# Where an expert's third block does its activation, and three small branches in place of one in the first three experts

## The chip, the cores and the metric

The kernel runs on one core of one Trainium2 chip. The metric is device time in microseconds (us), from three runs; the profile shows one further execution. Line numbers (L1286) are those of the kernel before.

## The reference, cut to what matters

Two blocks of a transformer run one after the other on 256 tokens of width 1024. The first block ends in a mixture of 32 experts: a router picks four experts for each token, and each expert computes, for its tokens only,

```python
hdn = xb @ w_gate_up[e] + b_gate_up[e]          # 1024 -> 2048
x_glu = jnp.minimum(hdn[..., :1024], 7.0)
x_lin = jnp.clip(hdn[..., 1024:], -7.0, 7.0)
a = x_glu * sigmoid(1.702 * x_glu) * (x_lin + 1)
y = a @ w_down[e] + b_down[e]                    # 1024 -> 1024
out[token] += y * gate
```

All weights are float32, 12 MiB for an expert. The second block (two feed-forward layers and a mixer) follows and is not touched by the change.

## The kernel before

The experts run in a loop that is unrolled over e = 0 to 31. An expert's weights come in six chunks of 2 MiB: gate-up chunks ("gu", e, 0 to 3), each 256 input rows, and down chunks ("dn", e, 0 and 1), each 512 rows. The chunks go through a ring of nine slots, eight from the second expert's down chunks on. SyncE (SP) issues their loads in a fixed order. `release(key)` tells the ring, at that place of the program, that a chunk has been read; `fill()` then writes the load that takes over the slot into SP's queue, and on the chip that load waits until TensorE (PE) has passed the last instruction that reads the old chunk. A load thus starts only after the chunk eight places ahead of it has been read for the last time in the program's order, whichever branch was taken.

How many tokens an expert has is known only on the chip. PE, ScalarE (ACT) and VectorE (DVE) each read the count v and branch:

- v at most 32: the small way (`many.Else()`), here called few: 32 rows, four column groups of PE at a time (`gate_up_q`, `act_q`, `down_s`).
- v over 32: the main way, here called many: 64 rows, two column groups (`gate_up`, `act`, `actT`, `down`).
- v over 64 (`SL`): many, and in an inner branch a third block for tokens 65 to 96 (`gather_q`, `gate_up_q`, `act_q`, `down_q`, `combine`). (Experts with over 96 tokens have a loop of their own, `rounds`, which this input does not enter.)

In the profiled execution experts 9, 13 and 20 have a third block; 0, 3, 4, 6, 11, 12, 14, 19 and 23 are many without one; the other twenty are few.

An expert has two branches. The first holds gate-up chunks 0 to 2 (for e = 0 to 2 it is three branches, one for each chunk). Between the branches the next expert's rows are gathered (L1114). The second holds gate-up chunk 3, the activation, `between()` (the next expert's transposes and the sums of a finished pair of experts), and both down chunks; in an expert with over 64 tokens the third block's remainder comes behind the main down product: gate-up rows 6 and 7 of the eight (L1259), its activation, its one-hot rows (`slots_q`, DVE) and their transposes (`sgT`), a down product of 32 instructions 512 columns wide in the one shared PSUM buffer "rot" (L1315), a copy, and eight products into the sums (L1221). Only behind the whole second branch stand `release` for gate-up chunk 3 and both down chunks:

```python
        release(("gu", e, 3))
        for j in range(2):
            release(("dn", e, j))
```

An inner branch that is not taken is stepped over; PE then counts its semaphores as though the branch had run.

Of the kernel before, what the change touches and what calls it, by code (L numbers as in the profile page):

```python
# [95 lines left out]
def build(tc, A, out, dbg=None):  # L96
# [115 lines left out]
    def chunk(key):  # L212
        return tiles[index[key]]
# [910 lines left out]
    def sgT(Sg, r=0, pool=None):  # L1124
# [3 lines left out]
        s = (pool or pe).tile([128, T], F32, name="SgT" + ("z" if r else ""), bufs=1)  # L1128
# [57 lines left out]
    def down(e, py, at, r=0):  # L1186
        for c in range(2):
# [10 lines left out]
        if r:  # L1198
            y = pe.tile([128, 512], F32, name="yz", bufs=1)
            nc.scalar.activation(y, py, AF.Copy)  # L1200
            return y

# [33 lines left out]
    def gather_q(e, xe, p):  # L1236
# [5 lines left out]
        x = pe.tile([128, T], F32, name="SgTz", bufs=1)  # L1242
# [28 lines left out]
    def down_s(e, at, py):  # L1271

        lse = sel[0:96, e:e + 1].to_broadcast([96, 32])
        for g in range(4):
            nc.tensor.matmul(py[32 * g:32 * g + 32, 0:T], lhsT=lse, rhs=bg[0:96, 2048 + T * g:2048 + T * g + T],
                             start=True, stop=False, skip_group_check=True)
        l = yield
# [4 lines left out]
        for c in range(2):  # L1282
            w = chunk(("dn", e, c)).rearrange("p (k f) -> p k f", k=4)
            for j in range(4):
                for g in range(4):
                    nc.tensor.matmul(py[32 * g:32 * g + 32, 0:T], lhsT=at[:, j, 32 * c:32 * c + 32],  # L1286
                                     rhs=w[:, j, T * g:T * g + T], start=False, stop=(c == 1 and j == 3),
                                     skip_group_check=True)
        o = 64 * (e % 2)
        for g in range(4):  # L1290
            d, q = pair["y"][o:o + 32, T * g:T * g + T], py[32 * g:32 * g + 32, 0:T]
# [4 lines left out]
        yield  # L1296

    def down_q(e, l):
        p = ps.tile([128, 4, 64], F32, name="rot", bufs=1)
        for j in range(4):  # L1300
            nc.tensor.transpose(p[:, j], l[:, 128 * j:128 * j + 128], ident[0:64, 0:64])
        at = pe.tile([128, 4, 64], F32, name="aTq")
        nc.scalar.activation(at, p, AF.Copy)
        st = sgT(slots_q(e, 4, [128, 2, 128], "Sgz", 1), 1)
        p = ps.tile([128, 512], F32, name="rot", bufs=1)
        lse = sel[0:96, e:e + 1].to_broadcast([96, 32])
        for o in range(2):
            nc.tensor.matmul(p[64 * o:64 * o + 32], lhsT=lse, rhs=bg[0:96, 2048 + 512 * o:2560 + 512 * o], start=True,
                             stop=False, skip_group_check=True)
        for j in range(4):  # L1310
            for o in range(2):
# [742 lines left out]
```

## Time and profile before

| what | value |
|---|---|
| time, median of 3 runs | 1770.94 us (1769.97 to 1772.21) |
| the profiled execution, its own time | 1769.94 us |
| its span, first to last instruction | 1768.1 us |
[...]
| PE, DVE, ACT busy | 85%, 44%, 30% |
| HBM read | 545.25 MB, 309 GB/s over the span |

PE's share is an average over stages with different limits. The stage of the experts runs from about 213 to 1196 us, the second block from there to the end. The row of GB/s in 40 slices (44.2 us each) shows in which of them the loads set the pace. A wait "<-issue" is time in which the engine waited for nothing that the profile shows. [...]

### The profile page before, as it was taken

The page shows a single profiled execution, that of the slowest core. Times are in us where ns is not written, and L with a number is a line of the kernel's source. Part 1 is how long each engine was busy: PE and PEld are TensorE (multiplying, and loading weights), DVE is VectorE, ACT ScalarE, POOL GpSimd, SP SyncE. Part 2 cuts the span into 40 slices and gives each one's busy share as a digit, 9 for nine tenths or more (in the row PEclk, how much of TensorE's full clock was granted, in tenths as well). Part 3 has the DMA queues.
Part 4 walks back from the last instruction along what each step waited for, and adds up shares of the span by engine and source line. Part 5 has one row for each costly group of instructions (what it writes and reads, how often), then busy time and mean ns, then how long its engine had stood idle before and what let it go on. Part 6 is the DMA issues. An engine that isn't in the chain of part 4 may idle for free. (4 is left out here: it accounts for less than half of the span.)

```text
span 1768.1 us, 26974 instructions
## 1 busy us (share of the span) xinstructions
PE 1501.6 (85%) x10842; PEld 984.5 (56%) x10842; DVE 779.3 (44%) x1605; ACT 522.3 (30%) x1114; POOL 106.5 (6%) x114
## 2 busy tenths in 40 slices
PE   6999978967779888778868776668999999999998
PEld 5787623323233332332323222227999989999997
DVE  5776613233332432433211111115766767676665
ACT  4544311101011010110101101005544556565444
POOL 3501100000000000000000000002000100310000
PEclk8999999998999999999979888889999999999999
DMA  9878779999999979999999999995554553344630
GB/s 353 323 229 340 277 271 414 417 415 416 416 401 412 413 290 366 415 415 417 406 383 402 409 416 416 416 414 218 191 205 159 193 201 144 143 165 170 221 137 25
DMA packets 89049, 549.49 MB, mean 311 GB/s; under 512 B 5064, under 2 KB 7912, under 8 KB 49448
## 3 DMA queue, kind: packets, MB, share of 16 engines
q1 hardware_dynamic: 88424, 544.55, 77.9%
q8 instruction: 154, 2.52, 0.6%
q0 software_dynamic: 272, 0.92, 0.2%
q10 hardware_dynamic: 144, 1.05, 0.2%
q14 instruction: 55, 0.45, 0.1%
HBM read 545.25 MB, written 1.25 MB: 309 GB/s over the span
## 5 line engine op out<-in xcount | busy, mean ns | idle before, releaser
L251 DVE TENSOR_TENSOR wl<-ring,wh 128x512 fp32r<-128x512 f32 x421 | 284.9, 710 | 114.8 <-ACT wh L250 108.1
L250 ACT ACTIVATE wh<-ring 128x512 fp32r<-128x512 f32 x424 | 248.7, 622 | 106.5 <-PE gu L281 86.1
L1259 PE MATMUL h<-ring,xe 128*32 128x512 f32 x1280 | 194.5, 733 | 56.4 <-DMA ring<-in_w_gate_up 32.4
L280 PE MATMUL gu<-ring,wh 128*128 128x256 f32 x704 | 201.2, 286 | 2.9 <-ACT ring L1586 2.9
L281 PE MATMUL gu<-ring,wh 128*128 128x256 f32 x704 | 200.4, 285 | 1.9 <-DVE ring L1590 1.9
L282 PE MATMUL gu<-ring,wl 128*128 128x256 f32 x704 | 200.4, 285 | 0.0
L1155 PE MATMUL h<-ring,xe 128*64 128x512 f32 x768 | 173.6, 594 | 11.4 <-DMA ring<-in_w_gate_up 9.8
L1259 PEld LDWEIGHTS h<-ring,xe 128*32 128x32 f32 x1280 | 50.4, 127 | 181.5 <-issue 145.8
L1264 DVE TENSOR_SCALAR glu<-h 64x512 f32<-64x512 f32 x23 | 15.7, 683 | 287.5 <-PE h L1259 287.5
L280 PEld LDWEIGHTS gu<-ring,wh 128*128 128x128 f32 x704 | 135.9, 193 | 3.5 <-ACT ring L1586 3.3
L281 PEld LDWEIGHTS gu<-ring,wh 128*128 128x128 f32 x704 | 135.9, 193 | 2.2 <-DVE ring L1590 2.1
L282 PEld LDWEIGHTS gu<-ring,wl 128*128 128x128 f32 x704 | 135.9, 193 | 0.0
L1117 ACT ACTIVATE xg<-rot 128x512 f32<-128x512 f32 x28 | 16.7, 597 | 381.4 <-PE rot L1114 381.4
L1155 PEld LDWEIGHTS h<-ring,xe 128*64 128x64 f32 x768 | 56.6, 137 | 113.1 <-issue 96.5
L280 PE MATMUL pd<-acth,wh 128*128 128x256 f32 x352 | 98.8, 281 | 0.1
L281 PE MATMUL pd<-actl,wh 128*128 128x256 f32 x352 | 98.3, 279 | 0.1
L282 PE MATMUL pd<-acth,wl 128*128 128x256 f32 x352 | 98.2, 279 | 0.0
L1286 PE MATMUL h<-ring,aT 128*32 128x256 f32 x1280 | 78.2, 394 | 21.2 <-ACT aT L1281 10.7
L1195 PE MATMUL h<-ring,aT 128*64 128x512 f32 x384 | 86.7, 605 | 6.4 <-ACT aT L1175 6.4
L1372 DVE COPY_PREDICATED bias<-bm,vecs 128x512 f32<-128x512 uint8 x124 | 80.0, 726 | 1.1
L1160 DVE TENSOR_SCALAR glu<-h 128x512 f32<-128x512 f32 x12 | 8.3, 692 | 160.6 <-PE h L1155 160.6
L280 PE MATMUL gu<-big_h,wh 128*128 128x256 f32 x256 | 74.6, 291 | 0.0
(446 smaller groups left out, 2450.2 us busy)
## 6 DMA issues: line engine op xcount, KB each, us to landing
ring<-in_w_gate_up SPq DMA_DIRECT2D x127, 2048.0 KB, 23.2
ring<-in_w_down SPq DMA_DIRECT2D x62, 2048.0 KB, 24.6
ring<-in_ffn_gu SPq DMA_DIRECT2D x22, 2048.0 KB, 8.0
ring<-in_win SPq DMA_DIRECT2D x12, 2048.0 KB, 8.2
ring<-in_ffn_wd SPq DMA_DIRECT2D x10, 2048.0 KB, 9.5
ring<-in_ada SPq DMA_DIRECT2D x8, 2048.0 KB, 11.5
ring<-in_wout SPq DMA_DIRECT2D x4, 2048.0 KB, 7.8
ring<-in_ada SPq DMA_DIRECT2D x4, 1024.0 KB, 12.4
```

The source lines that it names most:

```text
L250: nc.scalar.activation(dh, src, AF.Copy)
L251: (eng or nc.vector).tensor_tensor(dl, src, dh.bitcast(F32), op=OP.subtract)
L280: nc.tensor.matmul(o, lhsT=wh, rhs=mh, start=start, stop=False, skip_group_check=True)
L281: nc.tensor.matmul(o, lhsT=wh, rhs=ml, start=False, stop=False, skip_group_check=True)
L282: nc.tensor.matmul(o, lhsT=wl, rhs=mh, start=False, stop=stop, skip_group_check=True)
L1117: nc.scalar.activation(x, p, AF.Copy)
L1155: nc.tensor.matmul(p[64 * hf:64 * hf + 64], lhsT=x, rhs=wk[:, 512 * hf:512 * hf + 512], start=False, stop=(k == KD - 1), skip_group_check= ...
L1195: nc.tensor.matmul(py[64 * oh_:64 * oh_ + 64], lhsT=at[:, j, 64 * c:64 * c + 64], rhs=wk[:, 512 * oh_:512 * oh_ + 512], start=False, stop= ...
L1259: nc.tensor.matmul(p[32 * g:32 * g + 32], lhsT=x(k), rhs=w[:, k % 2, c], start=False, stop=(k == KD - 1), skip_group_check=True)
L1264: nc.vector.tensor_scalar(g, p[0:64], 7.0, None, op0=OP.min)
L1286: nc.tensor.matmul(py[32 * g:32 * g + 32, 0:T], lhsT=at[:, j, 32 * c:32 * c + 32], rhs=w[:, j, T * g:T * g + T], start=False, stop=(c == 1 ...
L1372: nc.vector.copy_predicated(bias2[:, h], m, val[:, :, None].to_broadcast([128, 2, T]))
```

## The change

For every expert: the third block's gate-up rows 6 and 7 and its activation move from behind the main down product to just behind the main activation; its one-hot rows with their transposes move into the first branch, behind gate-up rows 0 to 5; its down product is made by the few way's routine, in quarters: 64 instructions of 256 columns in four column groups, written into the third block's own PSUM buffer `pq` instead of "rot"; chunk dn 0 is read wholly before dn 1; its copy and its sums work on 256 columns and 32 rows.

For e = 0 to 2 alone: the second branch becomes three, one up to the activation's transposes, and one for each down chunk, with a `release` behind each. For e above 2 there is one second branch as before, with two inner branches in it instead of one.

```diff
-    def sgT(Sg, r=0, pool=None):
+    def sgT(Sg, r=0, pool=None, s=None):
...
-        s = (pool or pe).tile([128, T], F32, name="SgT" + ("z" if r else ""), bufs=1)
+        if s is None:
+            s = (pool or pe).tile([128, T], F32, name="SgT" + ("z" if r else ""), bufs=1)
...
-        x = pe.tile([128, T], F32, name="SgTz", bufs=1)
+        x = pe.tile([128, 512], F32, name="yz", bufs=1)[:, 0:T]
...
+    def down_q(e, at, p, cs):
+
+        for c in cs:
             w = chunk(("dn", e, c)).rearrange("p (k f) -> p k f", k=4)
             for j in range(4):
                 for g in range(4):
-                    nc.tensor.matmul(py[32 * g:32 * g + 32, 0:T], lhsT=at[:, j, 32 * c:32 * c + 32],
+                    nc.tensor.matmul(p[32 * g:32 * g + 32, 0:T], lhsT=at[:, j, 32 * c:32 * c + 32],
                                      rhs=w[:, j, T * g:T * g + T], start=False, stop=(c == 1 and j == 3),
                                      skip_group_check=True)
...
-        st = sgT(slots_q(e, 4, [128, 2, 128], "Sgz", 1), 1)
-        p = ps.tile([128, 512], F32, name="rot", bufs=1)
...
-        for j in range(4):
-            for o in range(2):
-                for c in range(2):
-                    w = chunk(("dn", e, c)).rearrange("p (k f) -> p k f", k=4)
-                    g = 64 * o + 32 * c
-                    nc.tensor.matmul(p[g:g + 32], lhsT=at[:, j, 32 * c:32 * c + 32],
-                                     rhs=w[:, j, 512 * o:512 * o + 512], start=(c == 1 and j == 0), stop=(j == 3),
-                                     skip_group_check=True)
+    def combine_q(p, s):
         y = pe.tile([128, 512], F32, name="yz", bufs=1)
-        nc.scalar.activation(y, p, AF.Copy)
-        return y, st
+        nc.scalar.activation(y[:, 0:T], p[:, 0:T], AF.Copy)
+        for k in range(KD):
+            g, i = k // 2, k % 2
+            nc.tensor.matmul(acc[k], lhsT=y[32 * g:32 * g + 32, 128 * i:128 * i + 128], rhs=s[32 * g:32 * g + 32, :],
+                             start=False, stop=False, skip_group_check=True)
...
                     gate_up_q(e, further, pq, ks)
+                    if js[-1] == 2:
+                        sgT(slots_q(e, 4, [128, 2, 128], "Sgz", 1), 1, None, sz)
...
-        with tc.If(v > 32) as many:
+        def many_a():
             gate_up(e, xe, pg, pl_, (3,))
             a = act(pg, pl_)
+            with tc.If(v > SL):
+                gate_up_q(e, further, pq, range(6, 8))
+                act_q(pq, lq)
             between()
             down_bias(e, pl_)
             actT(a, at)
-            down(e, pl_, at)
+
+        def many_b(cs):
+            down(e, pl_, at, 0, cs)
             with tc.If(v > SL):
-                gate_up_q(e, further, pq, range(6, 8))
-                act_q(pq, lq)
-                combine(*down_q(e, lq))
-        with many.Else():
+                if cs[0] == 0:
+                    turn_q(lq, az)
+                    bias_q(e, pq)
+                down_q(e, az, pq, cs)
+                if cs[-1] == 1:
+                    combine_q(pq, sz)
+
+        def few_a():
             gate_up_q(e, few, pg, range(6, 8))
             l = pe.tile([128, 512], F32, name="lin", bufs=1)[0:64]
             act_q(pg, l)
             between()
-            d = down_s(e, at, pl_)
-            next(d)
-            d.send(l)
+            bias_q(e, pl_)
+            turn_q(l, at)
+
+        def few_b(cs):
+            down_q(e, at, pl_, cs)
+            if cs[-1] == 1:
+                rows_q(e, pl_)
+
+        if e < 3:
+            with tc.If(v > 32) as many:
+                many_a()
+            with many.Else():
+                few_a()
+            release(("gu", e, 3))
+            for c in range(2):
+                with tc.If(v > 32) as many:
+                    many_b((c,))
+                with many.Else():
+                    few_b((c,))
+                release(("dn", e, c))
+        else:
+            with tc.If(v > 32) as many:
+                many_a()
+                many_b((0, 1))
+            with many.Else():
+                few_a()
+                few_b((0, 1))
+            release(("gu", e, 3))
+            for c in range(2):
+                release(("dn", e, c))
```

`turn_q`, `bias_q` and `rows_q` are the pieces of the old `down_s` (transposes and copy of the activation; the bias products; the copies of the result), with the same instructions.

## Rows read from the trace of the kernel before

**Rows 1.** The page, part 2: GB/s in 40 slices of 44.2 us.
```profile
GB/s 353 323 229 340 277 271 414 417 415 416 416 401 412 413 290 366 415 415 417 406 383 402 409 416 416 416 414 218 191 205 159 193 201 144 143 165 170 221 137 25
```

**Rows 2.** Chain that ended last, 1020 to 1210 us: start, us, what.
```profile
1033.87 54.87 DMA ring<-in_w_gate_up x2
```

**Rows 3.** Stretches: length, busy us by engine, PE clock, DMA share, GB/s.
```profile
234.00:248.00 14.00, 9.97 (x40) 3.34 (x39) 2.67 (x6) 1.83 (x4) 0.00 (x0) 0.88 0.17 56
...
268.50:272.00 3.50, 3.50 (x36) 1.58 (x32) 0.00 (x0) 0.00 (x0) 0.00 (x0) 0.50 1.00 413
...
625.00:692.00 67.00, 58.70 (x320) 22.93 (x320) 17.26 (x35) 8.26 (x18) 0.95 (x1) 0.95 0.77 302
700.00:875.00 175.00, 138.13 (x994) 54.31 (x990) 62.79 (x127) 20.88 (x49) 2.85 (x3) 0.95 1.02 416
875.00:975.00 100.00, 70.05 (x492) 28.21 (x484) 13.27 (x31) 10.28 (x24) 1.90 (x2) 0.89 0.97 389
```

**Rows 4.** Timeline of expert 0's second branch (start, us, engine, line, operation).
```profile
229.82 3.65 PE L1155 MATMUL h<-ring,xe 128*64 128x512 f32 x16
...
237.95 8.78 PE L1195 MATMUL h<-ring,aT 128*64 128x512 f32 x32 [0.47 <-ACT aT L1175]
...
246.87 5.83 SPq L208 DMA_DIRECT2D ring<-in_w_gate_up  x4
```

**Rows 5.** L208, the single loads issued at 246.9 and at 273.2 us.
```profile
DMA to landing us min/median/max: 8.6/8.6/8.6
...
DMA to landing us min/median/max: 14.3/14.3/14.3
```

**Rows 6.** PE's timeline, experts 1 and 2.
```profile
253.92 1.92 PE L1259 MATMUL h<-ring,xe 128*32 128x512 f32 x16 [1.65 <-issue]
...
261.15 2.60 PE L1259 MATMUL h<-ring,xe 128*32 128x512 f32 x16 [2.02 <-issue]
...
268.23 5.74 PE L1286 MATMUL h<-ring,aT 128*32 128x256 f32 x64 [0.53 <-ACT aT L1281]
...
276.94 3.63 PE L1259 MATMUL h<-ring,xe 128*32 128x512 f32 x28 [0.18 <-issue]
...
291.07 3.66 PE L1286 MATMUL h<-ring,aT 128*32 128x256 f32 x64 [0.53 <-ACT aT L1281]
```

**Rows 7.** Timeline of expert 13's second branch, PE and ACT, to expert 14's first product.
```profile
632.05 3.60 PE L1155 MATMUL h<-ring,xe 128*64 128x512 f32 x16
...
639.43 7.09 PE L1195 MATMUL h<-ring,aT 128*64 128x512 f32 x32 [0.53 <-ACT aT L1175]
646.45 1.92 PE L1259 MATMUL h<-ring,xq 128*32 128x512 f32 x16
...
651.50 0.66 PE L1301 MATMUL rot<-c,lq 64*128 64x64 f32 x4 [3.13 <-DVE poz L1227]
652.20 0.38 ACT L1303 ACTIVATE aTq<-rot 128x256 f32<-128x256 f32 x1 [2.41 <-PE rot L1301]
...
653.87 5.96 PE L1315 MATMUL rot<-ring,aTq 128*32 128x512 f32 x32
...
660.57 2.00 PE L1221 MATMUL acc<-SgTz,yz 64*128 64x256 f32 x16 [0.75 <-ACT yz L1319]
662.50 0.41 PE L1145 MATMUL h<-bg,sel 96*64 96x512 bf16 x2
```

**Rows 8.** Timeline of expert 14 (many, no third block), PE and SP.
```profile
674.18 1.94 PE L1114 MATMUL rot<-bias,S 128*64 128x512 f32 x8 [0.75 <-PEq L1479]
675.92 3.63 PE L1155 MATMUL h<-ring,xe 128*64 128x512 f32 x16
...
690.54 0.37 SPq L208 DMA_DIRECT2D ring<-in_w_down  x1
```

**Rows 9.** PE's timeline: expert 9's chunk 2, and the first products of expert 10.
```profile
482.51 3.65 PE L1155 MATMUL h<-ring,xe 128*64 128x512 f32 x16 [1.32 <-DMA ring<-in_w_gate_up]
...
530.45 0.65 PE L1256 MATMUL h<-bg,sel 96*32 96x512 bf16 x4 [4.32 <-issue]
```

More of the change, by code (lines that the diff above doesn't have):

```diff
@@ L1184, in down_bias, with down @@
         return py
-    def down(e, py, at, r=0):
-        for c in range(2):
+    def down(e, py, at, r=0, cs=(0, 1)):
+        for c in cs:
             w = None if r else chunk(("dn", e, c)).rearrange("p (k f) -> p k f", k=4)
@@ L1201, in down @@
             return y
+        if cs[-1] == 0:
+            return
         o = 64 * (e % 2)
@@ L1269, in act_q, with turn_q @@
         nc.vector.tensor_mul(l, l, s)
[L1271 to L1277, printed above, removed]
+    def turn_q(l, at):
         p = ps.tile([128, 4, 64], F32, name="rot", bufs=1)
@@ L1281, in down_s, with bias_q @@
         nc.scalar.activation(at[:, :, 0:64], p, AF.Copy)
-        for c in range(2):
+    def bias_q(e, p):
+        lse = sel[0:96, e:e + 1].to_broadcast([96, 32])
+        for g in range(4):
+            nc.tensor.matmul(p[32 * g:32 * g + 32, 0:T], lhsT=lse, rhs=bg[0:96, 2048 + T * g:2048 + T * g + T],
+                             start=True, stop=False, skip_group_check=True)
+    def down_q(e, at, p, cs):
+        for c in cs:
             w = chunk(("dn", e, c)).rearrange("p (k f) -> p k f", k=4)
@@ L1285, in down_s, with rows_q @@
                 for g in range(4):
-                    nc.tensor.matmul(py[32 * g:32 * g + 32, 0:T], lhsT=at[:, j, 32 * c:32 * c + 32],
+                    nc.tensor.matmul(p[32 * g:32 * g + 32, 0:T], lhsT=at[:, j, 32 * c:32 * c + 32],
                                      rhs=w[:, j, T * g:T * g + T], start=False, stop=(c == 1 and j == 3),
                                      skip_group_check=True)
+    def rows_q(e, p):
         o = 64 * (e % 2)
         for g in range(4):
-            d, q = pair["y"][o:o + 32, T * g:T * g + T], py[32 * g:32 * g + 32, 0:T]
+            d, q = pair["y"][o:o + 32, T * g:T * g + T], p[32 * g:32 * g + 32, 0:T]
             if g % 2:
@@ L1295, in down_s @@
                 nc.scalar.activation(d, q, AF.Copy)
-        yield
-    def down_q(e, l):
-        p = ps.tile([128, 4, 64], F32, name="rot", bufs=1)
-        for j in range(4):
-            nc.tensor.transpose(p[:, j], l[:, 128 * j:128 * j + 128], ident[0:64, 0:64])
-        at = pe.tile([128, 4, 64], F32, name="aTq")
-        nc.scalar.activation(at, p, AF.Copy)
-        st = sgT(slots_q(e, 4, [128, 2, 128], "Sgz", 1), 1)
-        p = ps.tile([128, 512], F32, name="rot", bufs=1)
-        lse = sel[0:96, e:e + 1].to_broadcast([96, 32])
-        for o in range(2):
[L1308 to L1311, printed above, removed]
-                for c in range(2):
-                    w = chunk(("dn", e, c)).rearrange("p (k f) -> p k f", k=4)
-                    g = 64 * o + 32 * c
-                    nc.tensor.matmul(p[g:g + 32], lhsT=at[:, j, 32 * c:32 * c + 32],
-                                     rhs=w[:, j, 512 * o:512 * o + 512], start=(c == 1 and j == 0), stop=(j == 3),
-                                     skip_group_check=True)
-        y = pe.tile([128, 512], F32, name="yz", bufs=1)
-        nc.scalar.activation(y, p, AF.Copy)
-        return y, st
+    def combine_q(p, s):
+        y = pe.tile([128, 512], F32, name="yz", bufs=1)
+        nc.scalar.activation(y[:, 0:T], p[:, 0:T], AF.Copy)
[3 more added lines that the diff above has]
+                             start=False, stop=False, skip_group_check=True)
     bias2 = keep2.tile([128, 4, 2, T], F32, name="bias2")
@@ L1459, in build @@
         lq = pe.tile([64, 512], F32, name="lq")
+        az = pe.tile([128, 4, 64], F32, name="aTq")
+        sz = pe.tile([128, T], F32, name="SgTz", bufs=1)
         at = pe.tile([128, 4, 128], F32, name="aT", bufs=1)
@@ L1519, in build @@
         xe = xn
-        release(("gu", e, 3))
-        for j in range(2):
-            release(("dn", e, j))
         if nxt:
```

## The prediction, made before the changed kernel ran

> **What bounds the kernel now.** I read the GB/s by slices first [rows 1]. In the experts' stage the loads run at 413 to 417 GB/s wherever nothing disturbs them, and the chain of waits near the end of the stage is little but loads, one piece of it 54.87 us of gate-up chunks [rows 2]. A chunk of 2 MiB (2.097 MB) takes 5.04 us at 416 GB/s [rows 3]. So the stage ends when its 192 chunks are through, and it loses time only where the loads stand still. What to look for is therefore a low rate in the table of stretches. It falls in three places [rows 3]: 234 to 248 us moves 56 GB/s, a loss of 14 x (1 - 56/416) = 12.1 us; 625 to 692 us moves 302, a loss of 18.4 us; 875 to 975 us moves 389, a loss of 6.5 us.
>
> In each hole the loads wait for PE to hand back a slot. In expert 0 PE reads gate-up chunk 3 for the last time at 233.47 us (229.82 + 3.65), but SP issues the load into its slot at 246.87, when the whole second branch is over [rows 4]: the third block, which is not even taken there, is in the program's order the last reader of all three held chunks. A load into an empty queue lands 8.6 us after its issue [rows 5], against 5.04 us behind another, so each halt costs a start-up besides. In experts 9 to 14 PE itself is late: expert 13's part behind the main down product lasts from 646.45 to 662.50 us, 16.05 us [rows 7], and expert 14's chunk 3, read by 679.55, is handed back at 690.54 [rows 8].
>
> After expert 14 PE waits for loads again, and after the experts the second block starts when the last chunk is used, so a microsecond saved in a hole should reach the end.
>
> **The change, part by part.**
>
> *First three experts.* Expert 0: the load now issued at 246.87 can start at about 234.0 (233.47 and 0.5 for stepping over the inner branch) and lands at 242.6 instead of 255.5 [rows 4, 5]. The next needs dn 0 read: the down product starts at 237.95, and I add 0.5 us for the new branch; half of its 8.78 us, the slower half, is about 5.4, so 243.9, landing at 252.5. The third follows at 257.6. Then expert 1 sets the pace, on PE. Its down product starts at 268.23 [rows 6], and I put the two new branches ahead of it at 1.2 us late together: 269.4. Dn 0 is then read by 272.8 (half of 5.74 at half the clock, somewhat over 2.87), and expert 3's first chunk, issued at 273.0, lands at 281.7. Before it was issued at 273.2 and landed 14.3 us later [rows 5], at 287.5, behind a queue that the hole had made late. That would be 5.8 us; that expert 1's own chunk 3 may be handed back only at the end of its activation costs up to 2, and I take 4.0 us. Bounds: nothing (PE late by 6 more, below) and 5.8. PE pays for the added branches, but it waits for loads before expert 9 anyway (1.32 us at one chunk there [rows 9]), which absorbs them.
>
> *The third block.* By expert 13 [rows 7]. Gate-up ends at 635.65. The moved rows 6 and 7 take 1.92 us of PE behind it, while DVE is at the main activation. Some of that may be hidden in the 3.78 us up to the down product, but `between` and the main transposes fill most of these, so I add all of it and 0.5 for the inner branch: the down product starts at 639.43 + 2.4 = 641.9 and ends, 7.0 us later, at 648.9. The third block's activation is by then done on DVE; the 3.13 us that PE waited for it, the transposes of the one-hots and a copy between them are gone. What is left: transposes (0.66 before) and their copy of 0.38, which stands behind the main result's copy on ACT, 1.2 us in all; 64 instructions of 256 columns in 3.66 us, as the few way has them [rows 6]; a copy of 0.4 and the sums in 2.0: 656.1 instead of 662.50, 6.4 us earlier. The one-hots are now in PE's way in the first branch: by the rows of the block's other transposes and copy, 0.66 and 0.38, it is 1.0 us until "rot" is free for the next gather. With 0.2 for the second inner branch each third block gains 5.2 us. [...] Bounds 2.2 to 6.4. Two third blocks, 9 and 13, lie in the stretch that PE bounds (expert 20 is counted below): 10.4 us.
>
> *Stepping over.* Experts 11, 12 and 14 now step over an inner branch between gate-up and the sums as well. Leaving the first branch costs 0.75 us with an inner branch stepped over and one jump [rows 8]; I take 0.4 each, 1.2 us lost. Bounds 0 and 2.2.
>
> *Chunk 3 handed back early* in every expert over 32 tokens with e above 2. PE passes its last reading straight behind gate-up chunk 3: in expert 14 at about 680 instead of 690.54 [rows 8]. The halt around it (the load lands 8.6 us after its issue, some 2 us behind the queue) goes: 1.9 us.
>
> *875 to 975 us.* Expert 20's third block ends 5.2 us earlier, and expert 23's chunk 3 comes back some 11 us earlier, as in expert 14: of the 6.5 us lost there [rows 3] I take 4.9, bounds 0 and 6.5.
>
> *Entries of branches.* PE pays for reaching the far side of a long branch: 4.32 us idle ahead of expert 10 [rows 9], 1.65, 2.02 and 0.18 in experts 1 and 2 [rows 6]. The main side grows by 32 instructions of the down product, and expert 10 stands in the bound stretch; in experts 0 to 2 six entries are new. Beyond the 1.2 us above I take 2.5 us. Bounds 0 and 10. [...]
>
> Sum: 4.0 + 10.4 - 1.2 + 1.9 + 4.9 - 2.5 = 17.5 us. The profiled execution's own time is 1769.94 us, 1.0 below the median of the runs; 1769.9 - 17.5 = 1752.4, and I predict 1752.5. About 0.2%, 3.5 us, is what a measurement of this kernel can tell from no change.
>
> **Rivals.**
>
> *Only part of it.* The moved gate-up rows and activation are not hidden: ACT runs the third block's sigmoid ahead of the copies that the main transposes wait for, the main down product starts 5 us later instead of 2.4, and the last product still runs at half clock. Each third block then gains about 0.5 us. For it: ACT and "rot" serve both chains in order. Against it: of the moved work only the 1.92 us are PE's, and the sigmoid, a single instruction, waits for DVE no longer than PE is busy with `between`. Time: 17.5 - 2 x 4.7 - 2 = 6.1 gained, 1764.
>
> *The first branches bring nothing.* Experts 3 to 8 have no hole, so what is won ahead of them counts only if expert 9 takes it over; if PE is by then the later one, the 4.0 are lost: 1756.5. For it: the added branches cost PE, and its waits ahead of expert 9 are short.
>
> *No change.* The holes only move: loads go ahead, the ring is empty sooner, and PE's long entries [rows 9] still set when slots come back. Time 1768 to 1771. Against it: after 700 us the loads run at 416 GB/s with PE waiting.
>
> [...]
>
> **How the numbers follow.** The sum, within 1746 to 1760: 0.60, which takes in the first branches bringing nothing (0.15 of it). Only part of it: 0.20. No change: 0.07. Slower by the entries: 0.07; the remaining 0.06 is more than the sum, down to 1742, with every bound on the good side. Range for 8 in 10: 1745 to 1766, leaving out the two last rivals and the far good end. Faster by over 0.2%: 0.60 + 0.20 + 0.06 = 0.86; within: 0.07; slower: 0.07.
>
> **What would show it.** The first three: a load issued near 234 us and no stretch at 56 GB/s. The third block: 64 instructions of about 3.7 us together, gate-up rows 6 and 7 ahead of the main down product, and some 20.5 us instead of 26.85 from the end of expert 13's main gate-up to expert 14's first product. The early hand-back: a down chunk's load issued right behind gate-up chunk 3 in expert 14, not at its end. The holes of 625 to 692 and 875 to 975 us shrink from 18.4 and 6.5 to under 10 and 2. The prediction is wrong if the early hand-back does not take place in branches that step over the third block, or if waits "<-issue" at L1259 and L1286 of experts 0 to 2 exceed 4 us together.

## The result: slower, and what the profile after shows

The changed kernel takes 1781.99 us (median of 7 runs, 1776.25 to 1786.89); the kernel before took 1770.08 us beside it. The ratio is 1.0059, 95% interval 1.0044 to 1.0073: 11.9 us slower, where 17.5 faster was forecast. The profiled execution of after took 1783.6 us, its span is 1781.8 us.

The page of after, GB/s in 40 slices (44.5 us each) and the gate-up line of the few way (L1262, the former L1259):

```profile
GB/s 360 320 225 332 282 356 388 360 405 416 415 376 381 381 328 346 416 414 417 414 374 382 397 417 413 416 413 257 189 176 180 189 207 142 142 152 181 213 142 24
...
L1262 PE MATMUL h<-ring,xe 128*32 128x512 f32 x1280 | 202.4, 754 | 76.1 <-issue 74.4
```

Against [rows 1] the hole of the sixth slice is filled (271 GB/s before, 356 now), and new ones have opened: 388, 360, 376, 381, 374. In a load-bound stage this means that PE has become late. Its waits say where. Each row: the waiting line, what released it, us in total, times, the longest. First before, 213 to 1197 us:

```profile
PE h L1259 <- DMA ring<-in_w_gate_up: 32.4, 18, 3.1
PE h L1259 <- issue: 23.9, 12, 3.7
```

and after, 214 to 1211 us:

```profile
PE h L1262 <- issue: 74.4, 23, 4.6
PE h L1259 <- issue: 39.7, 7, 11.2
...
PE h L1292 <- issue: 3.8, 2, 2.0
```

The waits of this line for loads are all but gone (one of 1.7 us is left), and 50 us of waits for nothing that the profile shows have come in their place. One of them is the entry of a few expert (15) into its second branch. PE's timeline of after (start, us, engine, line, operation, idle time before it):

```profile
713.29 1.94 PE L1114 MATMUL rot<-bias,S 128*64 128x512 f32 x8
719.59 2.73 PE L1262 MATMUL h<-ring,xe 128*32 128x512 f32 x12 [4.35 <-issue]
```

The gather ends at 715.2, and PE does nothing for 4.35 us, released by no load and no engine: it has jumped over the whole main side to reach the few side. The jump itself stands in the trace, as a branch of PE's sequencer (PEldq) at L1539, the `If` of the second branch (shortest, median and longest in ns, then when):

```profile
L1539 PEldq COMPARE_BRANCH  x1: 6088/6088/6088, 713.3 to 713.3; - x1
```

It takes 6.09 us; the gather's product, which was already under way, covers the first 1.9 of them, and the rest is the gap. All branches at this `If`, before (L1498) and after (from expert 3 on):

```profile
L1498 PEldq COMPARE_BRANCH  x32: 73/378/6284, 229.2 to 1180.6; - x32
L1539 PEldq COMPARE_BRANCH  x29: 73/426/6197, 317.4 to 1193.7; - x29
```

Five of the 32 take over 6 us before, thirteen of the 29 take 5.9 to 6.2 us after. These thirteen, of the eighteen few experts behind expert 2, let PE stop for 4.1 to 4.6 us; in the kernel before no wait of this line is over 3.7 us. In the first 1.5 us of products behind these thirteen stops the granted clock is 0.50 to 0.85 of full speed, in eight of them 0.50 to 0.56. The stretch behind the one above (busy us by engine, then PE clock, DMA share, GB/s):

```profile
719.60:722.30 2.70, 2.70 (x16) 0.68 (x16) 0.00 (x0) 0.00 (x0) 0.00 (x0) 0.52 1.04 434
```

The other rows that answer to those of before. Stretches, against [rows 3]:

```profile
234.00:248.00 14.00, 10.46 (x42) 3.21 (x38) 2.21 (x5) 1.28 (x4) 0.00 (x0) 0.88 0.83 315
625.00:692.00 67.00, 61.50 (x391) 23.33 (x388) 23.12 (x50) 7.45 (x17) 0.95 (x1) 0.97 0.88 349
...
875.00:975.00 100.00, 68.60 (x521) 27.82 (x518) 15.79 (x36) 9.69 (x23) 0.95 (x1) 0.86 0.95 381
```

Expert 0's early load, SP's queue, against [rows 4], and PE in experts 1 and 2, against [rows 6]:

```profile
234.59 21.34 SPq L208 DMA_DIRECT2D ring<-in_w_gate_up  x4
```

```profile
253.59 3.64 PE L1262 MATMUL h<-ring,xe 128*32 128x512 f32 x32 [2.31 <-issue]
...
272.60 3.58 PE L1292 MATMUL h<-ring,aT 128*32 128x256 f32 x32 [1.81 <-issue]
279.06 0.43 PE L1259 MATMUL h<-bg,sel 96*32 96x512 bf16 x4 [2.89 <-DVE aTz L1328]
...
284.98 1.92 PE L1262 MATMUL h<-ring,xe 128*32 128x512 f32 x16 [0.36 <-issue]
...
302.08 2.52 PE L1292 MATMUL h<-ring,aT 128*32 128x256 f32 x32 [1.97 <-issue]
...
305.57 1.06 PE L1156 MATMUL h<-ring,xe 128*64 128x512 f32 x2
```

The load issued at 246.87 now leaves at about 234.6, as forecast, and the stretch went from 56 to 315 GB/s. But PE's waits for issue at these two lines are 2.31 + 1.81 + 0.36 + 1.97 = 6.5 us in experts 1 and 2, against 1.65 + 2.02 + 0.18 = 3.9 [rows 6], two of them at new entries (the second down chunk's), and 2.89 us ahead of expert 2 besides. Expert 3 begins at 305.57 instead of 296.7. Expert 13, against [rows 7]:

```profile
645.83 3.60 PE L1156 MATMUL h<-ring,xe 128*64 128x512 f32 x16
649.37 1.92 PE L1262 MATMUL h<-ring,xq 128*32 128x512 f32 x16
...
655.06 7.09 PE L1196 MATMUL h<-ring,aT 128*64 128x512 f32 x32 [0.53 <-ACT aT L1176]
...
663.25 3.66 PE L1292 MATMUL h<-ring,aTq 128*32 128x256 f32 x64 [0.48 <-ACT aTq L1278]
667.46 1.17 PE L1310 MATMUL acc<-SgTz,yz 32*128 32x256 f32 x16 [0.55 <-ACT yz L1307]
668.56 0.41 PE L1146 MATMUL h<-bg,sel 96*64 96x512 bf16 x2
```

From the end of the main gate-up (649.43) to expert 14's first product (668.56) there are 19.1 us instead of 26.85: the third block itself does what the change was made for. Expert 10's first product, behind the third block of expert 9, against [rows 9]:

```profile
537.98 0.65 PE L1259 MATMUL h<-bg,sel 96*32 96x512 bf16 x4 [7.84 <-issue]
```

And expert 14, over 32 tokens without a third block, against [rows 8]: PE as it reads chunk 3 for the last time, and SP as it issues the next loads.

```profile
684.96 3.94 PE L1156 MATMUL h<-ring,xe 128*64 128x512 f32 x16
...
693.11 7.09 PE L1196 MATMUL h<-ring,aT 128*64 128x512 f32 x32 [0.53 <-ACT aT L1176]
```

```profile
680.73 19.87 SPq L208 DMA_DIRECT2D ring<-in_w_down  x2
```

Chunk 3 is read for the last time at 688.90, but the second of SP's two loads leaves at 700.2, when the whole branch is over (700.20): no early hand-back. SP's waits, 640 to 720 us, give its releaser:

```profile
SPq L208 <- PEq L1505: 19.1, 1, 19.1
```

L1505 is the second inner branch, which PE steps over behind the main down product.

### The profile page after: what moved, and what is told of

The parts are those of the page before. It is cut to its first block, busy times and chain, and to the rows that moved or that the text cites. A ratio compares the mean times of both kernels' runs of the same rounds, so it can differ in the third digit from the quotient of the medians.

```text
span 1781.8 us, 27263 instructions
## 1 busy us (share of the span) xinstructions
PE 1517.7 (85%) x10944; PEld 997.8 (56%) x10944; DVE 779.7 (44%) x1605; ACT 521.2 (29%) x1114; POOL 106.6 (6%) x114
## 5 line engine op out<-in xcount | busy, mean ns | idle before, releaser
L251 DVE TENSOR_TENSOR wl<-ring,wh 128x512 fp32r<-128x512 f32 x421 | 285.0, 711 | 114.6 <-ACT wh L250 107.8
L1262 PE MATMUL h<-ring,xe 128*32 128x512 f32 x1280 | 202.4, 754 | 76.1 <-issue 74.4
L1262 PEld LDWEIGHTS h<-ring,xe 128*32 128x32 f32 x1280 | 55.7, 129 | 194.8 <-issue 189.7
L282 PE MATMUL gu<-big_h,wl 128*128 128x256 f32 x256 | 71.5, 279 | 1.1 <-DVE wl L251 1.1
```

Of the source, the lines that this page charges most:

```text
L251: (eng or nc.vector).tensor_tensor(dl, src, dh.bitcast(F32), op=OP.subtract)
L282: nc.tensor.matmul(o, lhsT=wl, rhs=mh, start=False, stop=stop, skip_group_check=True)
L1262: nc.tensor.matmul(p[32 * g:32 * g + 32], lhsT=x(k), rhs=w[:, k % 2, c], start=False, stop=(k == KD - 1), skip_group_check=True)
```

## Experiments

Ratios are against the kernel before on the same chip, with their 95% intervals. Three more numbers are read from the timelines of each profiled execution: the start of expert 3's first gate-up product, the time from there to the end of the last expert's down product, and how long after the last reading of expert 14's chunk 3 the load into its slot is issued (hand-back).

| kernel | time, us | ratio | expert 3 at | from there | hand-back |
|---|---|---|---|---|---|
| before | 1770.1 | 1 | 296.7 | 899.7 | 11.0 |
| after | 1782.0 | 1.0059 (1.0044 to 1.0073) | 305.6 | 904.7 | 11.3 |
| e1_wide_third | 1761.6 | 0.9943 (0.993 to 0.9956) | 294.8 | 893.4 | 3.4 |
| e2_pad16 | 1782.3 | 1.0059 (1.0042 to 1.0076) | 306.5 | 901.7 | 11.0 |
| e3_third_only | 1768.9 | 0.9985 (0.9972 to 0.9997) | 304.1 | 893.7 | 11.2 |
| e4_split_only | 1768.4 | 0.9979 (0.9969 to 0.999) | 306.1 | 889.8 | 11.0 |
| e5_wide_nosplit | 1762.1 | 0.9952 (0.9939 to 0.9965) | 296.7 | 890.2 | 3.4 |
| e6_wide_pad16 | 1781.9 | 1.0061 (1.0048 to 1.0075) | 305.3 | 908.6 | 10.4 |
| e7_before_shift | 1769.5 | 0.9992 (0.9983 to 1.0) | 302.5 | 896.0 | 11.0 |
| e8_after_shift | 1773.4 | 1.0027 (1.0014 to 1.0039) | 294.9 | 904.9 | 11.2 |
| e9_apart | 1760.2 | 0.9943 (0.9929 to 0.9956) | 293.2 | 893.5 | 10.9 |
| e10_wide_between | 1798.4 | 1.0144 (1.0128 to 1.0161) | 306.3 | 919.8 | 3.4 |
| e11_apart_narrow | 1757.2 | 0.9928 (0.9914 to 0.9942) | 294.3 | 888.5 | 10.9 |
| e12_wide_shift | 1758.6 | 0.9932 (0.9918 to 0.9945) | 292.5 | 890.9 | 3.4 |
| e13_out | 1746.3 | 0.9858 (0.9836 to 0.9881) | 299.5 | 871.0 | 0.1 |
| e14_few_pad16 | 1786.2 | 1.0082 (1.0056 to 1.0107) | 305.4 | 911.9 | 0.1 |
| e15_out_nosplit | 1747.6 | 0.9865 (0.9849 to 0.9882) | 300.8 | 875.8 | 0.1 |
| e16_out_again | 1745.7 | 0.986 (0.9843 to 0.9876) | 299.2 | 873.0 | 0.1 |
| e17_out_late | 1760.2 | 0.9946 (0.9931 to 0.9962) | 300.1 | 886.9 | 11.3 |

My theory after the result (F): PE pays for the code that a jump passes over, and the narrow product, 64 instructions and 64 weight loads in place of 32 and 32, made the main side longer. With the product at its old length it asked for 1760 to 1770 us and for 75 to 95 us of PE's waits for issue over the stage.

**e1_wide_third**: the changed kernel with the third block's down product in 32 instructions of 512 columns, as before.

```diff
-                    bias_q(e, pq)
-                down_q(e, az, pq, cs)
+                    bias_w(e, pq)
+                down_w(e, az, pq, cs)
...
-                    combine_q(pq, sz)
+                    combine(y, sz)
```

> The changed kernel, but the third block's down product again as 32 instructions of 512 columns in two column groups, its copy and sums as before; all else as changed. [...] Rival B (branches): the second inner branch and the added branches cost by themselves; waits stay at 115 us or more and the time at 1776 to 1786. Rival S (first three): what experts 0 to 2 lose is carried to the end; the time stays within 4 us of the changed kernel.

1761.6 us: the narrow product costs 20.4 us, though only three experts execute it, and in those it is the faster of the two (3.66 us against 5.96 [rows 7]). The time is as theory F had it; its waits for issue were not: over the stage PE's add up to 107.8 us (128.3 in the changed kernel) where 75 to 95 was expected, 59.1 of them at L1262. The hand-back, which no theory had in view yet, moved too, to 3.4 us.

**e2_pad16**: the kernel before, with products in the third block that never run.

```diff
                 combine(*down_q(e, lq))
+                with tc.If(v > 250):
+                    for _ in range(16):
+                        nc.tensor.matmul(pq[0:32, 0:128], lhsT=ident[:, 0:32], rhs=ident, ...)
```

> The kernel before, with 16 more fp32 products on PE (64 instructions, as PE's fp32 products are counted in the trace with their weight loads) inside the third block, behind an inner branch that is never taken: nothing more is computed, only the main side is longer. Theory F: the waits of the changed kernel appear without its work: PE waits for nothing visible 105 to 135 us in the experts' stage, time 1776 to 1786 us. Rivals B and S: no expert without a third block runs one more branch, so 1768 to 1772 us.

1782.3 us, 11.5 slower, with not one instruction of work more (counted as the trace counts the ones that run, two products and two weight loads for each, the 16 are 64 instructions, as many as the narrow product adds): code that nobody executes is enough for the change's whole loss. But 9.8 us of it have arisen by expert 3, so place in memory could also be the reason, and PE's waits for issue come to 95.3 us, short of the 105 to 135 that theory F asked for.

**e3_third_only**: the changed kernel without the split of the second branch, `if e < 0:` for `if e < 3:`.

> The changed kernel with one second branch in experts 0 to 2 as in all others: all of the third block's change, none of the first three's. Theory F: the waits stay at 115 us or more, and the time at 1774 to 1783 us, a few us under the changed kernel at most. Rival S: 1762 to 1769 us. Rival B: between, 1772 to 1778 us.

**e4_split_only**: the split in experts 0 to 2 alone; from expert 3 on the second branch of the kernel before.

```diff
-        if e < 3:
+        if e < 0:                       # e3
...
+            if e < 3: many_b((c,))      # e4: the new third block in 0 to 2
+            else: combine(*down_old(e, lq))
```

> The changed code for experts 0 to 2 alone; from expert 3 on the second branch of the kernel before, with its third block behind the main down product. Theory F: only three experts are longer, so 1766 to 1774 us, PE's waits for nothing visible 75 to 90 us. Rival S: 1778 to 1784 us. Rival B: 1770 to 1774 us.

1768.9 and 1768.4 us: neither half alone is slower than before, both together are by 12. Theory F missed e3 (it asked for 1774 or more) and met e4. In e4 expert 3 begins 9.4 us late, but what follows takes 9.9 us less than before; its loads had run ahead (362 GB/s from 234 to 248 us, where before has 56).

The miss of e3 matters. From expert 3 on it has the changed kernel's code, only at another place and behind other loads. As many of its entries into the second branch are long (15, of 5.9 to 6.5 us), it waits longer at L1262 (83.0 us), it hands chunk 3 back as late, and yet it takes 893.7 us from there against 904.7. The difference lies in experts 3 to 10, which take 244.8 us against 257.0; there PE's branches of over half a microsecond add up to 23.3 us against 35.1, and it is at other `If`s than the second branch's that they are shorter. So which branches are long depends on more than their length, behind expert 2 too, and theory F by itself does not give what a jump costs.

**e5_wide_nosplit**: e1 without the split.

> The changed kernel with the third block's down product again 32 instructions of 512 columns and without the split second branches of experts 0 to 2. Theory F (what costs is the length of the main side that a jump passes, and the narrow product is the longest thing added to it): without the narrow product the main side is nearly as short as before, so the third blocks' gain stays and the time is 1757 to 1767 us, within 5 us of the same kernel with the split (1761.6); PE's waits for issue over the experts below 100 us. Rival S (each added entry of the split costs, and the third block's move brings little by itself): 5 to 10 us faster than with the split, under 1757. Rival A (what a jump costs hangs on where its target falls in the instruction memory, so every edit rolls dice): no forecast from length; 1760 to 1780, and no order between kernels with and without the split.

1762.1 against 1761.6: with the wide product the split neither costs nor gives anything.

**e6_wide_pad16**: e1 with the 16 products of e2 at the end of the third block, never run.

> The kernel with the wide third product and the split (1761.6 us), and behind the third block's sums an inner branch that is never taken, with 16 products of 128 columns in it that never run: the main side is as long as in the changed kernel, the executed work that of the wide one. Theory F (length): 1775 to 1785, as the changed kernel. [...] Rival A (place): anything between, with 1765 to 1775 the likeliest.

1781.9, as the changed kernel, with the executed work of the wide product: the narrow one costs by standing there, not by its execution. The hand-back went back to 10.4 us with it, so jump and hand-back are not told apart here.

**e7_before_shift, e8_after_shift, e12_wide_shift**: one never-taken branch ahead of expert 0 that moves all experts' code back, in the kernel before, the changed one and e1.

```diff
+        if e == 0:
+            with tc.If(v > 250):
+                for _ in range(32):
+                    nc.tensor.matmul(pq[0:32, 0:128], lhsT=ident[:, 0:32], rhs=ident, ...)
```

> The kernel before, with one inner branch ahead of expert 0 that is never taken, and in it 32 products of 128 columns that never run. No expert's code is longer; all of it only lies further back in the instruction memory, by the length of these. Theory F (length): same as before within 0.2%, 1768 to 1773. Rival A (place): more than 4 us off to one side, and the waits for issue move to other experts' branches.

> The changed kernel with the same never-taken branch of 32 products ahead of expert 0. Theory F (length): same as the changed kernel within 0.3%, 1776 to 1787. Rival A (place): more than 5 us off, and if it comes out under 1772 most of the change's loss was the place of its code and not its length.

> The kernel with the wide product and the split (1761.6), and ahead of expert 0 the never-taken branch of 32 products. By the changed kernel with and without it (8.6 us apart, all of it ahead of expert 3, where the one starts at 305.6 us and the other at 294.9), place decides in experts 1 and 2 and not behind them. Theory F with place in the first experts: expert 3 starts between 294 and 306 us, and what follows takes 893 us as without the shift, within 4 us; time 1760 to 1772. Rival A (place everywhere): what follows differs by over 6 us.

Place does matter, and theory F, which had none of it, failed in e8 (1773.4 us where it asked for 1776 or more). The shift is worth +5.8, -10.7 and -2.3 us by the start of expert 3. From there on the stage takes 896.0 against 899.7, 904.9 against 904.7 and 890.9 against 893.4 us. The kernel before makes 3.7 of its 5.8 us good there; the changed one keeps 8.6 us of what it wins. In e12 the stage behind expert 3 came out as forecast, but expert 3 (292.5 us) and the time (1758.6) lie below their ranges. e3 above shows that place, or the loads ahead, can count behind expert 3 as well.

**e9_apart, e11_apart_narrow**: the third block as a branch of its own behind the many/few branch in both halves, without split, with the wide and the narrow product.

```diff
         with tc.If(v > 32) as many:
...
-            with tc.If(v > SL):
-                gate_up_q(e, further, pq, range(6, 8))
...
         with many.Else():
...
+        with tc.If(v > SL):
+            gate_up_q(e, further, pq, range(6, 8))
+            act_q(pq, lq)
+            turn_q(lq, az)
...
```

> The third block taken out of the main side: in both halves it is a branch of its own behind the many/few branch, with the wide product, no split, its activation and all its second half behind the main down product, and only the one-hots moved into the first half. Every expert has two jumps more, but the jump over the main side is shorter by the whole third block. Theory F (a jump that passes the long main side stalls PE, a shorter one stalls it less): the few experts' entries fall from 6 to 2 us in most experts, PE's waits for issue below 75 us, time 1750 to 1762, although each third block is some 3 us longer than in the kernel with the wide product and no split (1762). Rival T (what limits is how fast instructions arrive in all, those of sides not taken included): the code is as long as with the third block inside, so no gain, 1762 to 1772. Rival J (each taken jump costs, however short): two jumps more in 28 experts, 1770 to 1785.

> The kernel with the third block as a branch of its own, with the narrow product of the changed kernel (64 more instructions in the third block). Theory F: the jump over the third block alone stays short, so the narrow product costs little, within 5 us of the same kernel with the wide product. Rival T: 10 us or more above it.

1760.2 and 1757.2 us, although nothing of the third block overlaps with the main one any more and chunk 3 comes back as late as before. There the narrow product costs nothing, its own shorter run in three experts (5.96 to 3.66 us in each) counted in. PE's waits in e9, 213 to 1187 us:

```profile
PE h L1262 <- DMA ring<-in_w_gate_up: 53.9, 28, 4.5
...
PE h L1262 <- issue: 13.8, 11, 3.3
```

PE waits for loads again. Every expert has jumps more, so rival J is out, and 64 instructions and loads more do not bring the 10 us that rival T asked for. But the trace does not show the reason that theory F gave, a jump that stays short: of 35 branches at the third block (L1525) 8 take over half a microsecond in e9 and 21 in e11, up to 5.8 us in both. In e11 PE still waits 43.4 us for loads, so a late PE costs less there.

**e10_wide_between and e14_few_pad16**: e1 with the 16 products that never run between two experts, and at the end of the few side.

> The kernel with the wide product and the split (1761.6), and the never-taken branch with 16 products of 128 columns not inside the main side but between two experts, ahead of the end of each. The code of every expert is as long as with the same products inside the third block (1781.9), the main side as short as without them. Theory F (length of the side that a jump passes): 1761 to 1768, nearer to the kernel without them. Rival T (all code that has to arrive, wherever it stands): 1776 to 1786. In the first three experts the place of the code may add up to 10 us to either.

> The kernel with the wide product and the split (1761.6), with the never-taken branch of 16 products at the end of the few side, which the 12 experts of over 32 tokens jump over. Theory F: those experts' exits stall, the idle time of PE between the down product of expert 3 and the first product of expert 4 grows from 1.5 us to 4 to 7 (it was 7.15 with the same products between the experts), the few experts' entries stay as without them; 1770 to 1790. Rival M (only the main side's length matters, through the few experts' entries): expert 3's exit stays at 1.5 us, the time within 5 us of 1761.6.

1798.4 and 1786.2 us. For e10 both forecasts failed: the main side is short and the code costs 36.8 us. Part of it lies at the exit of an expert over 32 tokens. PE in e1, experts 3 and 4:

```profile
315.69 7.09 PE L1196 MATMUL h<-ring,aT 128*64 128x512 f32 x32 [0.53 <-ACT aT L1176]
324.23 0.41 PE L1146 MATMUL h<-bg,sel 96*64 96x512 bf16 x2 [1.46 <-DVE wz L1212]
```

and in e14:

```profile
326.20 7.09 PE L1196 MATMUL h<-ring,aT 128*64 128x512 f32 x32 [0.53 <-ACT aT L1176]
340.20 0.64 PE L1146 MATMUL h<-bg,sel 96*64 96x512 bf16 x2 [6.91 <-DVEq L1488]
```

1.46 us have become 6.91 (7.15 in e10). The profile puts this wait down to DVE, but PE's own branch at this exit, over the few side, takes 6.05 us of it. It is the one long branch of 26 at its line in e14; the others stay under 1.6 us:

```profile
L1521 PEldq COMPARE_BRANCH  x26: 73/288/6050, 238.7 to 993.8; - x26
```

In e10 three of 31 branches over the added products take 5.7 to 5.8 us. So a jump over the few side can be long as well, and theory F had to be widened from "the main side"; but that is one exit of twelve in e14, and some 5 us of the 24.5 by which it is slower than e1. Some 11 us more, in both kernels, have arisen by expert 3, where place alone does as much. The rest of it is not accounted for. The few experts' entries stay no worse than in e1, as theory F asked for e14: 48.0 us of issue at L1262 in 14 waits, against 59.1 in 16.

**e13_out**: the changed kernel, with the second part of the third block behind the main side in a branch of its own; e16_out_again is the same kernel on another occasion.

```diff
         def many_b(cs):
             down(e, pl_, at, 0, cs)
-            with tc.If(v > SL):
+
+        def third_b(cs):
+            with tc.If(v > SL):
...
             with many.Else():
                 few_a()
                 few_b((0, 1))
+            third_b((0, 1))
             release(("gu", e, 3))
```

> The changed kernel itself (1782), with one edit: the third block's transposes, narrow product and sums stand behind the main side in a branch of their own and not inside it, in the split branches of experts 0 to 2 as well. Its gate-up, its activation and the one-hots stay where the change put them; no instruction of work is added or taken away. Theory F (what costs is how much code PE jumps over in one go; the narrow product made the main side too long to jump over): the few experts' entries come down and the time with them, to 1757 to 1768. Rival T (all code that has to arrive): 1776 to 1786, as the change. Rival J (each jump costs): above the change, 1783 to 1792, since every expert has a jump more.

> The same kernel as e13_out again, beside the one without the split: 1742 to 1753, to compare the two on one chip.

1746.3 and 1745.7 us: 36 us below the changed kernel with the same work, 11 below what theory F had asked for, and the best kernel of this study. The page of e13, and PE's waits, 214 to 1171 us:

```profile
GB/s 357 324 234 348 267 349 415 405 414 416 415 416 416 415 362 407 415 415 414 417 412 415 415 415 415 412 407 177 188 200 170 199 165 144 141 194 155 229 126 25
```

```profile
PE h L1259 <- issue: 68.8, 13, 13.0
...
PE h L1262 <- DMA ring<-in_w_gate_up: 13.1, 9, 2.5
...
PE h L1262 <- issue: 9.5, 6, 3.3
```

At L1262 74.4 us of issue have become 9.5. At L1259, where a few expert enters its first branch, they have grown from 39.7 to 68.8; in all, PE's waits for issue over the stage fall from 128.3 to 84.7 us. The branches at the second `If` (now L1542) and at the new branch of the third block (L1507, all of them and the one of expert 14):

```profile
L1542 PEldq COMPARE_BRANCH  x40: 65/308/2021, 310.9 to 1153.6; - x40
L1507 PEldq COMPARE_BRANCH  x38: 71/340/5863, 238.1 to 1169.9; - x38
L1507 PEldq COMPARE_BRANCH  x1: 5837/5837/5837, 665.5 to 665.5; - x1
```

From expert 3 on no entry takes over 2.1 us any more. The jump over the third block is still long in places, but it now stands behind a long product: in expert 14 it begins at 665.5 us, while PE is busy with the main down product until 669.5, so that 4.0 of its 5.84 us cost nothing. Expert 14 and the few expert 15 on PE, and SP:

```profile
654.70 3.63 PE L1156 MATMUL h<-ring,xe 128*64 128x512 f32 x16
...
662.44 7.09 PE L1196 MATMUL h<-ring,aT 128*64 128x512 f32 x32 [0.53 <-ACT aT L1176]
...
685.56 1.94 PE L1114 MATMUL rot<-bias,S 128*64 128x512 f32 x8
687.43 1.92 PE L1262 MATMUL h<-ring,xe 128*32 128x512 f32 x16
```

```profile
653.29 5.53 SPq L208 DMA_DIRECT2D ring<-in_w_down  x2
```

```profile
687.50:689.30 1.80, 1.80 (x17) 0.36 (x17) 0.00 (x0) 0.60 (x1) 0.00 (x0) 1.00 1.00 414
```

The entry of expert 15 into its second branch has no gap, its products run at a granted 1.00 (the last row, a stretch), and the load into chunk 3's slot leaves by 658.8, right behind the reading that ends at 658.33: the early hand-back of the prediction, which the changed kernel does not have.

**e15_out_nosplit**: e13 without the split of experts 0 to 2.

> The kernel of the run before with the third block's second part in a branch of its own (1746), without the split second branches of experts 0 to 2. Theory F: the split pays its entries in experts 1 and 2 (down products of 8.9 and 5.7 us there, against 5.7 and 3.7 in the kernel before) and gives expert 0's early loads; both are a few us and about cancel: 1741 to 1752. Rival S (the split's early loads are worth the 4.0 us that the prediction gave them): 1749 to 1756, slower than with it. Rival E (the entries of the split cost more than it gives): under 1743.

1747.6 against 1745.7 us on the same chip; the intervals of the ratios overlap. By the medians the split is worth 2.0 us, which these runs do not tell from nothing.

**e17_out_late**: e13, with a product that never runs and would read chunk 3 at the end of the new branch.

```diff
                     combine_q(pq, sz)
+                    if e > 2:
+                        with tc.If(v > 250):
+                            nc.tensor.matmul(pq[0:32, 0:128], lhsT=ident[:, 0:32],
+                                             rhs=chunk(("gu", e, 3))[:, 0:128], ...)
```

> The kernel with the third block's second part in a branch of its own (1746), with one product more at the end of that branch in experts from 3 on, in an inner branch that is never taken: it reads gate-up chunk 3, so that the chunk is handed back only behind this branch, some 11 us later, as in the kernel before and in the changed one. The jumps stay as short. Theory H (half of the mended kernel's gain is the early hand-back): 1751 to 1760. Theory F alone (the jumps' length is all of it): 1744 to 1750.

1760.2 us. SP in e17, and PE's waits, 213 to 1187 us:

```profile
661.95 16.74 SPq L208 DMA_DIRECT2D ring<-in_w_down  x2
```

```profile
PE h L1262 <- issue: 16.8, 9, 3.4
```

One of the two theories was that short jumps are all of it; it falls. Late hand-back costs 14 us, at the upper end of theory H. For the hand-back that the prediction had in view this is an upper bound: in the three experts with a third block it comes 19 us after the main reading and not 12.7, and in the few expert 15, for one, 9.7 us after it, as against 4.8 in e13 and 0.0 in the changed kernel.

## Why the prediction was wrong

Two of its steps failed, and it had named both as what would make it wrong.

*Entries of branches*, taken at 2.5 us with bounds of 0 and 10, was mis-sized. The changed kernel and e17 have the same work and the same split, and e17 hands chunk 3 back no earlier (11.3 us in expert 14 in both, later in others); still they differ by 1782.0 - 1760.2 = 21.8 us. What differs in their traces is the jump over the third block's second part, inside the main side in one and by itself in the other: thirteen entries of 5.9 to 6.2 us against none over 1.9, and waits for issue at L1262 of 74.4 us against 16.8. Of the 21.8 us 5.5 have arisen by expert 3, where place alone does as much; and against e3, which has as many long entries and no split, e17 is only 8.7 us faster (6.9 by the ratios). So the term measures some 7 to 22 us, by place, where 2.5 was taken. The prediction saw the 32 added products, but priced them as one longer entry behind expert 9. Every few expert has to jump over them, and thirteen took some 6 us for it where five had before. It looked for new stalls in the added branches of experts 0 to 2; the trace has 1.81 and 1.97 us at two of these and 4.1 to 4.6 us at thirteen others. Slower by the entries, the outcome that came, had a chance of 0.07.

The traces at expert 15: a branch of 6.09 us with 4.35 us of PE idle behind the jump in after, and no gap in e13, where no entry from expert 3 on takes over 2.1 us. What makes such a jump long, no run shows.

*Chunk 3 handed back early* (1.9 us, and part of the 4.9 us at 875 to 975) did not take place: 11.3 us in expert 14 as against 11.0 before. Where it takes place, it may be worth more than forecast: e17 against e13 and e16, 14 us at most. The stretches agree that the holes stayed, though after holds in them work from 7 to 15 us earlier in the program: 625 to 692 us loses 67 x (1 - 349/416) = 10.8 us and 875 to 975 us 100 x (1 - 381/416) = 8.4, where under 10 and under 2 were forecast.

*The third block* was right and somewhat too small: 5.2 us for each was forecast. Between the first products of expert 13 and of expert 14 lie 50.9 us before and 44.1 after, 6.8 us less with the one-hots in the first branch paid for; its product took 3.66 us, at a granted 1.00. *Stepping over* an inner branch: the time from gate-up to the down product grew from 3.8 to 4.1 us in the experts over 32 tokens without a third block, 0.1 less than the 0.4 taken.

*First three experts*: the loads went out early as forecast, the 4.0 us were not won, because PE took 8 us more from the start of the stage to expert 3. How much is lost there hangs on where the code lies (e8 has the same instructions and loses none of it). With the rest mended the split gives 2.0 us or nothing (e15, e16).

Where the expected gain went, in sum: the third block's gain is there, some 7 to 22 us of longer jumps cover it, and up to 14 us of the early hand-back did not come about. Without either loss the change gains 25 us (e16: 1771.2 to 1745.7).

What stays open: why the hand-back comes 0.1, 3.4, 10.4 or 11 us after the last reading, in kernels that differ by code that never runs or stands elsewhere. Never-run code on the main side made it later (3.4 in e1, 10.4 in e6), on the few side earlier (0.1 in e14), and taking the third block's product out of the main side earlier too (11.3 to 0.1). The reason was not traced. Nor was what decides which of several jumps of one length is long (the place effect, e3 against the changed kernel), nor why e10 and e14 lose so much. The first branches were not mended either: their branches of over half a microsecond add up to 75.6 us in e13, against 10.5 in e9, where the third block stands apart in that half too; the two together were not run.

## What to carry to other kernels

Count the instructions that a branch makes an engine jump over, those that are hardly ever executed above all: in e6 16 products that never run made the kernel 20.2 us slower than e1. Here a rare block did best in a branch of its own behind the common sides, where the jump over it runs while a long product is still at work (4.0 of 5.84 us in expert 14 of e13), and not inside one of them (1746.3 us against 1782.0). Look in the trace for the branch instructions and how long each took, and not only for the gaps behind them. When a kernel with branches is changed, read the entries of the side that was not touched. And when a buffer is to come free earlier, look in the trace which instruction releases the load into it, since a reading that is over did not hand it back by itself here (in expert 14 of after the load left 11.3 us behind the last reading).

## What the runs showed of the hardware

A branch of PE took from 0.07 us to over 6 us: at the second `If` of after the median of 29 is 0.43 us and the longest 6.20, with thirteen of 5.9 to 6.2 us, and of e13, with less code to pass over, the longest is 2.02. PE's products already under way cover part of such a branch (1.9 of 6.09 us at expert 15 of after, 4.0 of 5.84 us in expert 14 of e13), so that the gaps behind it were 4.1 to 4.6 us in after, and 6.91 us at one exit of e14. The products behind the gap of 4.35 us ran at a granted 0.52 over 2.7 us; in e13, where PE had not stood still, they ran at 1.00.

Sixteen products that never run, in one branch of each expert, made the kernel 11.5 us slower in e2, 20.2 in e6, 24.5 in e14 and 36.8 in e10, of which 10 to 12 us each time ahead of expert 3; the narrow product's instructions cost nothing in a branch of their own (e11 against e9, 3 us faster). Moving all code by one never-taken branch of 32 products shifted the start of expert 3 by up to 10.7 us and left the rest of the stage within 4 us; the same code from expert 3 on, at another place and behind other loads, took 893.7 us in e3 and 904.7 in after.
